# Gathers begin in the table's stage, table parts of 16 tokens, U chunks spread over V's loop

## The chip, the cores and the metric

The kernel runs on one core of a Trainium2 chip. The metric is device time in microseconds, from the first to the last instruction of one launch with what lies around them. Of several executions the median is taken.

## What is computed

One decoder layer for 512 tokens of width 1024, in float32: a sliding-window attention and an HGRN2 recurrence, merged, and then a PEER layer, which is what the change touches. For each token and each of 8 heads PEER finds 16 of 16384 experts by a product of two 128-key tables, with gates from a softmax. Each expert is one row of U and one row of V:

```python
def expert_block(args):
    ht, it, gt = args                       # tokens, expert numbers (128 a token), gates
    ue = jnp.take(u, it, axis=0)
    act = jax.nn.gelu(jnp.einsum('tkd,td->tk', ue, ht), approximate=False)
    ve = jnp.take(v, it, axis=0)
    return jnp.einsum('tk,tkd->td', gt * act, ve)
```

U and V have 16384 x 1024 elements, 64 MB each. The layer's output goes through a residual and a final RMS norm.

## The kernel before

**Two ways through PEER.** For 352 of the 512 tokens the kernel computes all experts densely. U comes in 128 chunks of 128 experts (`act_chunk`: a 512 KB load `s<-uc`, ScalarE makes `hi`, VectorE makes `lo`, PE does 24 matmuls of 128x352 at lines 642 to 645, ScalarE's Gelu at line 647 leaves 128 experts x 352 tokens in `gel`). The split in `hi` and `lo`, both of type fp32r, keeps the products' accuracy near float32. The gates stand in a table `Gd` in DRAM, expert by token, zero where a token did not choose the expert. V comes in 128 chunks as well: `w` is `gel` times the table (line 958), split in `whi` and `wlo`, and 18 matmuls of 512 columns (lines 972 to 974) add the chunk to six accumulators that stay in PSUM through the whole loop.

For the other 160 tokens the kernel gathers. 320 steps (`steps`, line 678) each fetch 128 rows, 512 KB, with an indirect DMA from GpSimd (line 687) into one of four `ga` buffers. A step on U takes a row's product with its token on VectorE (line 695); a step on V adds the row with its weight (line 705). `pace(goal, after)` issues gathers until `goal` have gone and puts each product two gathers behind.

**The stages.** Up to about 390 us the mixers run, then routing, in which 24 U chunks fill PE. From 612 to 782 us comes the table's stage (lines 873 to 897): for 8 tokens at a time VectorE makes one-hots `oh` in four operations, PE multiplies them (line 891, 16 matmuls), ScalarE moves the result to `G_`, and every 32 tokens (a part, 2 MB, 11 in all) SP writes the part to `Gd`. Between them U chunks are slotted in by `fill`. The buffers `gel` hold 53 chunks (`KEEP`); of these 50 are asked for before the read of the table's first slice (`g_load`), three after it (`LASTU`). Then comes V's loop (line 951): each of 128 steps does one V chunk, one U chunk as long as there are any, and gathers in proportion to PE's work. So the first 75 steps have a U chunk each and the last 53 have none.

**What sets the order.** The program is recorded in the order of the code, and a scheduler places each instruction on its engine's queue by a model of readiness, recorded order deciding between those that are ready; `issue_after` binds an instruction behind another, `keep_in_program_order` keeps the gathers in theirs. On the chip each engine takes its queue strictly in order. Buffers that matter: three for U loads (`s`), two for V loads (`vr`), two for `hi` and `lo`, which U and V share, two for `oh`, two for `G_`, four for `ga`, two PSUM banks for U chunks. SP's queue issues all loads and the table's writes.

## Time and profile before

| | us |
|---|---|
| median of three runs | 1681.73 (1674.09 to 1688.14) |
| profiled execution, its own time | 1682.85 |
| its span, first to last instruction | 1680.8 |
| PE busy | 1612.4 (96%) |
| VectorE busy | 1316.3 (78%) |
| ScalarE busy | 712.5 (42%) |
| GpSimd busy | 472.3 (28%) |
| moved by DMA | 400.88 MB, mean 238 GB/s |

An engine's busy share over the whole span hides stages with different limits, so the rows below are taken stage by stage. PEclk is the granted clock of PE as a share of full speed. The DMA share is the mean over 16 DMA engines; around 1.00 they are saturated. A wait is put down to what came last.

### The profile page before, as it was taken

How to read it: one execution, taken by the hardware profiler on the slowest of the kernel's cores; microseconds unless marked ns; L12 is line 12 of the kernel's file. 1: busy time of each engine (PE TensorE's matmuls, PEld its weight loads, DVE VectorE, ACT ScalarE, POOL GpSimd, SP SyncE). 2: the span in 40 equal slices, each digit the busy share in tenths (PEclk: the TensorE clock that was granted, in tenths of full speed). 3: DMA queues.
4: the chain of work that ended last, by engine and by line, in shares of the span. 5: the costliest groups of instructions: out<-in, count | busy, mean ns of one | idle time of the engine just before them, and what ended most of it. 6: DMA issues, size and time to landing. Idle time of an engine off the chain costs nothing.

```text
span 1680.8 us, 23572 instructions
## 1 busy us (share of the span) xinstructions
PE 1612.4 (96%) x8511; PEld 1357.3 (81%) x8511; DVE 1316.3 (78%) x2560; ACT 712.5 (42%) x1152; POOL 472.3 (28%) x341
## 2 busy tenths in 40 slices
PE   8999999999999989998899999999999999998997
PEld 6867678888989889997788888888888888776665
DVE  8466663647999988784888888888888887987788
ACT  5433352345455567775333333333333333333334
POOL 4000000000000000001455555555555554554442
PEclk9999999999999999999899999999999999999999
DMA  5311133324333236668999999999999998899985
GB/s 172 113 39 51 51 113 113 113 104 142 118 107 116 103 102 201 207 201 247 350 356 347 353 359 357 358 337 362 380 363 358 354 346 298 324 341 345 336 312 192
DMA packets 152260, 400.88 MB, mean 238 GB/s; under 512 B 13056, under 2 KB 60672, under 8 KB 152144
## 3 DMA queue, kind: packets, MB, share of 16 engines
q1 hardware_dynamic: 104064, 229.09, 39.8%
q0 software_dynamic: 46336, 168.39, 26.4%
q10 hardware_dynamic: 1744, 1.91, 0.4%
q8 instruction: 66, 1.08, 0.3%
q14 instruction: 50, 0.41, 0.1%
HBM read 371.91 MB, written 27.39 MB: 238 GB/s over the span
## 4 chain that ended last, share of the span: by engine, by line
PE 60%; DVE 15%; DMA 13%; issue 7%; POOL 3%; ACT 2%; DVEq 0%; ACTq 0%; SPq 0%; POOLq 0%
PE b L973 6%; PE b L974 6%; PE b L972 6%; PE b L642 5%; PE b L645 5%; PE b L643 5%; PE b L891 5%; DMA ga<-un,idx 5%; DMA vr<-vc 5%; PE b L262 4%; PE b L261 4%; DVE lo L161 4%; PE b L264 4%; DMA ga<-v,idx 3%; POOL ga L687 2%
## 5 line engine op out<-in xcount | busy, mean ns | idle before, releaser
L687 POOL DMA_INDIRECT ga<-un,idx x160 | 220.3, 1377 | 948.4 <-DMA s<-uc 753.0
L642 PE MATMUL b<-hT,hi 128*128 128x352 f32 x1024 | 330.2, 326 | 1.4 <-ACT hi L141 0.9
L643 PE MATMUL b<-hT,hi 128*128 128x352 f32 x1024 | 331.1, 325 | 0.0
L973 PE MATMUL b<-lo,whi 128*128 128x512 f32 (+1 forms) x768 | 307.6, 401 | 21.6 <-DVE lo L161 21.5
L972 PE MATMUL b<-hi,whi 128*128 128x512 f32 (+1 forms) x768 | 305.4, 399 | 19.1 <-ACT hi L141 18.9
L141 ACT ACTIVATE hi<-s 128x1024 fp32r<-128x1024 f32 (+1 forms) x195 | 205.8, 1056 | 264.9 <-PE b L643 161.4
L974 PE MATMUL b<-hi,wlo 128*128 128x512 f32 (+1 forms) x768 | 304.6, 397 | 0.0
L687 POOL DMA_INDIRECT ga<-v,idx x160 | 230.5, 1441 | 219.5 <-DVE e L705 202.6
L161 DVE TENSOR_TENSOR lo<-s,hi 128x1024 fp32r<-128x1024 f32 (+1 forms) x195 | 239.0, 1226 | 33.4 <-ACT hi L141 29.2
L141 ACT ACTIVATE whi<-w 128x352 fp32r<-128x352 f32 x128 | 63.5, 497 | 384.2 <-PE b L973 333.7
L705 DVE SCALAR_TENSOR_TENSOR e<-ga,wt,e 128x1024 f32<-128x1024 f32 x158 | 202.3, 1281 | 15.0 <-DMA ga<-v,idx 14.8
L695 DVE SCALAR_TENSOR_TENSOR dscr<-ga,h 128x1024 bf16<-128x1024 f32 x160 | 195.5, 1222 | 21.3 <-DMA ga<-un,idx 21.1
L642 PEld LDWEIGHTS b<-hT,hi 128*128 128x128 f32 x1024 | 193.1, 189 | 7.7 <-ACT hi L141 1.2
L973 PEld LDWEIGHTS b<-lo,whi 128*128 128x128 f32 (+1 forms) x768 | 139.4, 181 | 71.9 <-DVE lo L161 35.7
L643 PEld LDWEIGHTS b<-hT,hi 128*128 128x128 f32 x1024 | 193.4, 189 | 4.0
L645 PE MATMUL b<-hT,lo 128*128 128x352 f32 x1024 | 194.9, 326 | 0.0
L972 PEld LDWEIGHTS b<-hi,whi 128*128 128x128 f32 (+1 forms) x768 | 138.9, 181 | 58.6 <-ACT hi L141 25.0
L161 DVE TENSOR_TENSOR lo<-vr,hi 128x1024 fp32r<-128x1024 f32 x128 | 156.3, 1221 | 26.9 <-ACT hi L141 26.7
L974 PEld LDWEIGHTS b<-hi,wlo 128*128 128x128 f32 (+1 forms) x768 | 139.1, 181 | 38.9
L645 PEld LDWEIGHTS b<-hT,lo 128*128 128x128 f32 x1024 | 168.0, 189 | 0.0
L141 ACT ACTIVATE hi<-vr 128x1024 fp32r<-128x1024 f32 x128 | 134.3, 1049 | 65.7 <-DMA vr<-vc 64.4
L262 PE MATMUL b<-hT,hi 128*128 128x512 f32 (+1 forms) x376 | 146.5, 391 | 0.3 <-DVE hT L144 0.3
(286 smaller groups left out, 2170.9 us busy)
## 6 DMA issues: line engine op xcount, KB each, us to landing
s<-uc SPq DMA_DIRECT2D x128, 512.0 KB, 5.9
vr<-vc SPq DMA_DIRECT2D x128, 512.0 KB, 6.3
Gd<-G SPq DMA_DIRECT2D x11, 2048.0 KB, 9.4
gt<-Gd SPq DMA_DIRECT2D x32, 704.0 KB, 7.8
s<-wfm SPq DMA_DIRECT2D x30, 512.0 KB, 3.2
s<-wq SPq DMA_DIRECT2D x16, 512.0 KB, 3.3
s<-wmg SPq DMA_DIRECT2D x8, 512.0 KB, 3.3
s<-wout SPq DMA_DIRECT2D x8, 512.0 KB, 3.3
```

Source lines behind the costliest of these rows:

```text
L141: ACT.activation(dst, src, AF.Copy)
L161: (eng or V).tensor_tensor(lo[:, m], raw[:, m], hi[:, m].bitcast(F32), op=OP.subtract)
L262: PE.matmul(b, wh[:, k, :], rl(i), start=False, stop=False)
L642: PE.matmul(o, wh[:, k, :], zh[:, k, t], start=k == 0, stop=False)
L643: PE.matmul(o, wh[:, k, :], zl[:, k, t], start=False, stop=False)
L645: PE.matmul(o, wl[:, k, :], zh[:, k, t], start=False, stop=k == KD - 1)
L687: tc.keep_in_program_order(POOL.indirect_dma_start(out=t, out_offset=None, in_=a[src], in_offset=bass.IndirectOffsetOnAxis(ap=b.idx[:, j:j ...
L695: V.scalar_tensor_tensor(cur["scr"], t, 1.0, h20, op0=OP.mult, op1=OP.mult, accum_out=b.act[:, j:j + 1])
L705: V.scalar_tensor_tensor(b.ax, t, b.wt[:, j:j + 1], b.ax, op0=OP.mult, op1=OP.add)
L972: PE.matmul(acc[tb][hf][0:m, :], whi[:, t], vh[:, d], start=i == 0, stop=False)
L973: PE.matmul(acc[tb][hf][0:m, :], whi[:, t], vl[:, d], start=False, stop=False)
L974: PE.matmul(acc[tb][hf][0:m, :], wlo[:, t], vh[:, d], start=False, stop=i == NE - 1)
```

## The change

Five things are changed together.

- A part of the table has 16 tokens instead of 32 (`TG`): 22 writes of 1 MB, and in each the piece that lies together in DRAM is 256 bytes long instead of 512. `G_` shrinks by half.
- Gathers begin in the table's stage: the `ga` buffers have a pool of their own, opened before it, and `pace` is called after each part (one gather for two parts) and once with the goal 18 ahead of V's loop. The product with U's rows overwrites the gathered tile, in float32; before, it went to a scratch tile in bfloat16.
- U chunks are spread evenly over the first 116 steps of V's loop (`UEND`), and the share of gathers follows the count of V and U chunks.
- `FILLQ` 4 lets a U chunk follow every fourth quad of tokens instead of every fifth; `HELD` 5 and `LASTU` 2 change how many of the 53 chunks come where.
- The U chunks after the table are bound behind the last table matmul, the last two of them behind the issue of the table's first read as well, and V's first two loads are recorded ahead of that read.

```diff
@@ -37,7 +37,7 @@
 EQB = 1
 GS = 4096.0
 GC = 4
-TG = 32
+TG = 16
 QT = 4
 OT = 8
 LOOK = 26
@@ -48,11 +48,13 @@
 GLAG = 2
 GB = 4
 TAILC = 2
-HELD = 7
-LASTU = 3
+HELD = 5
+LASTU = 2
+EARLY = 18
+UEND = 116
 TL = 2
 F1 = 1.5
-FILLQ = 5
+FILLQ = 4
 
 
 def host(inp):
@@ -683,7 +685,7 @@
 
         def gather(i):
             b, src, j = steps[i]
-            t = cur["late"].tile([P, D], F32, tag="ga", bufs=GB, name=nm("ga"))
+            t = cur["ga"].tile([P, D], F32, tag="ga", bufs=GB, name=nm("ga"))
             tc.keep_in_program_order(POOL.indirect_dma_start(
                 out=t, out_offset=None, in_=a[src], in_offset=bass.IndirectOffsetOnAxis(ap=b.idx[:, j:j + 1], axis=0)))
             gq.append(t)
@@ -692,7 +694,7 @@
             t = gq.pop(0)
             b, src, j = steps[i]
             if src == "un":
-                V.scalar_tensor_tensor(cur["scr"], t, 1.0, h20, op0=OP.mult, op1=OP.mult, accum_out=b.act[:, j:j + 1])
+                V.scalar_tensor_tensor(t, t, 1.0, h20, op0=OP.mult, op1=OP.mult, accum_out=b.act[:, j:j + 1])
                 if j == b.w - 1:
                     ACT.activation(b.act, b.act, AF.Gelu)
                     V.tensor_tensor(b.wt, b.act, b.gate, op=OP.mult)
@@ -848,6 +850,7 @@
                 p_, c_ = slice(r * X, (r + 1) * X), slice(r * XG, (r + 1) * XG)
                 SP.dma_start(sp1.idx[p_, :], idxt[0:X, c_])
                 SP.dma_start(sp1.gate[p_, :], gta[0:X, 1, c_])
+        cur["ga"] = ps.enter_context(tc.tile_pool(name="gap", bufs=1, reuse_waits="tile"))
         cur["gel2"] = ps.enter_context(tc.tile_pool(name="gel2", bufs=1, reuse_waits="tile"))
 
 
@@ -883,21 +886,21 @@
                     V.tensor_tensor(oh[:, 0], ioq, row(iT[:, 0, t]), op=OP.is_equal)
                     V.tensor_tensor(oh[:, 2], ioq, row(iT[:, 1, t]), op=OP.is_equal)
                     V.tensor_tensor(oh[:, 1], oh[:, 2], row(g16[:, 0, t]), op=OP.mult)
-                    V.tensor_tensor(oh[:, 2], oh[:, 2], row(g16[:, 1, t]), op=OP.mult)
+                    last = V.tensor_tensor(oh[:, 2], oh[:, 2], row(g16[:, 1, t]), op=OP.mult)
                     for q in range(NQ):
                         b = bank((P, QT, P))
                         for i in range(QT):
                             for w in range(2):
-                                PE.matmul(b[:, i, :], oh[:, 0, q, :, i], oh[:, 1 + w, q, :, i], start=w == 0, stop=w == 1)
+                                lastg = PE.matmul(b[:, i, :], oh[:, 0, q, :, i], oh[:, 1 + w, q, :, i], start=w == 0, stop=w == 1)
                         m = o * OT + q * QT
                         ACT.activation(G_[:, :, m:m + QT].rearrange("p c t -> p t c"), b, AF.Copy)
                         k = (s_ * TG + m) // QT
                         if k % FILLQ == FILLQ - 1 and nu[0] < KEEP - HELD:
                             fill(1)
                 SP.dma_start(Gd.rearrange("g p s f -> s p g f")[s_], G_.rearrange("p (g c) t -> p g (c t)", c=GC))
+                pace((s_ + 1) // 2, last.ins)
         late = ps.enter_context(tc.tile_pool(name="late", bufs=1, reuse_waits="tile"))
         cur["late"] = late
-        cur["scr"] = late.tile([P, D], mybir.dt.bfloat16, name="dscr")
 
         acc = [[bank() for _ in range(2)] for _ in range(DB)]
         fold = late.tile([P, X], F32, name="fold")
@@ -914,13 +917,16 @@
         def g_load(g):
             if g < NE // GC:
                 gts[g] = late.tile([P, NPT, GC * TG], F32, tag="gt", bufs=2, name=nm("gt"))
-                SP.dma_start(gts[g], Gd[g])
-
-        fill(KEEP - nu[0] - LASTU)
-        g_load(0)
+                return SP.dma_start(gts[g], Gd[g])
+
+        with tc.issue_after(lastg.ins):
+            fill(KEEP - nu[0] - LASTU)
         for c in range(VPRE):
             v_load(c)
-        fill(LASTU)
+        g0 = g_load(0)
+        pace(EARLY, last.ins)
+        with tc.issue_after(lastg.ins), tc.issue_after(g0.ins):
+            fill(LASTU)
 
         def scale_of(ss, n):
             r = oc.tile([P, 1], F32, tag="ss", bufs=8, name=nm("rs"))
@@ -932,10 +938,11 @@
 
         def final_rows(y, add, t, n):
             s2_ = oc.tile([P, 2], F32, tag="s2_", bufs=4, name=nm("s2_"))
+            sq = s4([P, D])
             for hf in range(2):
                 d = slice(hf * 512, (hf + 1) * 512)
                 V.tensor_tensor(y[:, d], y[:, d], add[hf], op=OP.add)
-                ACT.activation(cur["scr"][0:n, d], y[:, d], AF.Square, accum_out=s2_[0:n, hf:hf + 1])
+                ACT.activation(sq[0:n, d], y[:, d], AF.Square, accum_out=s2_[0:n, hf:hf + 1])
             ss = oc.tile([P, 1], F32, tag="ss", bufs=8, name=nm("rs"))
             V.tensor_tensor(ss[0:n, :], s2_[0:n, 0:1], s2_[0:n, 1:2], op=OP.add)
             r = scale_of(ss[0:n, :], n)
@@ -945,9 +952,8 @@
                 (SP, ACT)[hf].dma_start(out[t:t + n, d], y[:, d])
 
         todo_u = NE - nu[0]
-        whole = 2.0 * todo_u + (NE - todo_u - TAILC)
+        nu0 = nu[0]
         ready = []
-        share = 0.0
         for c in range(NE):
             if c % GC == 0:
                 g_load(c // GC + 1)
@@ -973,8 +979,8 @@
                             PE.matmul(acc[tb][hf][0:m, :], whi[:, t], vl[:, d], start=False, stop=False)
                             PE.matmul(acc[tb][hf][0:m, :], wlo[:, t], vh[:, d], start=False, stop=i == NE - 1)
                 ready = []
-            share += 2.0 if nu[0] < NE else 1.0
-            fill(1)
+            fill(min(NE, nu0 + -(-todo_u * (c + 1) // UEND)) - nu[0])
+            share = (c + 1 + nu[0] - nu0) / (NE - TAILC + todo_u)
             if c == NE - 8:
                 ld = exp_ln_set()
                 yt = [e8([P, 2, D]) for _ in range(2)]
@@ -996,7 +1002,7 @@
                     bs.append(bank(tag="p"))
                     PE.matmul(bs[hf][0:X, :], fold[:, 0:X], sp1.ax[:, hf * 512:(hf + 1) * 512], start=True, stop=True)
                 final_rows(yx[0:X, :], [b[0:X, :] for b in bs], P, X)
-            pace(NS * share / whole, last.ins)
+            pace(EARLY + (NS - EARLY) * share, last.ins)
 
         while nsp[0] < NS:
             sparse(nsp[0])
```

Where the changed program's queues differ is shown at three places. Line numbers in its rows are those of the changed code (`s<-uc` at 153, `Gd` at 900).

SP's queue as the table's stage begins, before (`s` a U load, `Gd` a part's write):

```order
L849 DMA idx_3081<-idxt 32x32 x4
L151 DMA s_1103_6349<-uc 128x1024
L151 DMA s_1117_6449<-uc 128x1024
L897 DMA Gd<-G_5609 128x32x128
L151 DMA s_1130_6544<-uc 128x1024
L897 DMA Gd<-G_5744 128x32x128
L151 DMA s_1143_6642<-uc 128x1024
L151 DMA s_1156_6737<-uc 128x1024
L897 DMA Gd<-G_5912 128x32x128
```

The same place of the changed program:

```order
L851 DMA idx_3081<-idxt 32x32 x4
L900 DMA Gd<-G_5612 128x32x64
L900 DMA Gd<-G_5697 128x32x64
L900 DMA Gd<-G_5784 128x32x64
L900 DMA Gd<-G_5869 128x32x64
L900 DMA Gd<-G_5956 128x32x64
L900 DMA Gd<-G_6041 128x32x64
L900 DMA Gd<-G_6129 128x32x64
L153 DMA s_1097_6265<-uc 128x1024
L900 DMA Gd<-G_6214 128x32x64
L153 DMA s_1110_6353<-uc 128x1024
```

Before, U loads stand between the writes from the first part on; now seven writes stand in a row, and from there on loads and writes alternate. On PE the same shows as a stretch without U chunks, from the 22nd to the 41st of the 88 quads of tokens; 45 chunks precede the last table matmul, before it was 51.

VectorE's queue at the end of the table's stage, before (`lo` a split, `ga` a gathered tile, `gt` the table's slice):

```order
L885 TENSOR_TENSOR oh_7266<-oh_7266,g_5518 128x1024
L886 TENSOR_TENSOR oh_7266<-oh_7266,g_5518 128x1024
L161 TENSOR_TENSOR lo_7602<-s_1276_7599,hi_7601 128x1024
L958 SCALAR_TENSOR_TENSOR w_7639<-gel_3136,gt_7529 128x352
L958 SCALAR_TENSOR_TENSOR w_7712<-gel_3233,gt_7529 128x352
L963 TENSOR_TENSOR wlo_7643<-w_7639,whi_7641 128x352
L695 SCALAR_TENSOR_TENSOR dscr,act_3079<-ga_7696,h_62 128x1024
```

And in the changed program:

```order
L889 TENSOR_TENSOR oh_7447<-oh_7447,g_5521 128x1024
L697 SCALAR_TENSOR_TENSOR ga_7163,act_3079<-ga_7163,h_62 128x1024
L697 SCALAR_TENSOR_TENSOR ga_7334,act_3079<-ga_7334,h_62 128x1024
L697 SCALAR_TENSOR_TENSOR ga_7505,act_3079<-ga_7505,h_62 128x1024
L697 SCALAR_TENSOR_TENSOR ga_7622,act_3079<-ga_7622,h_62 128x1024
L697 SCALAR_TENSOR_TENSOR ga_7625,act_3079<-ga_7625,h_62 128x1024
L163 TENSOR_TENSOR lo_7304<-s_1245_7301,hi_7303 128x1024
L697 SCALAR_TENSOR_TENSOR ga_7628,act_3079<-ga_7628,h_62 128x1024
L697 SCALAR_TENSOR_TENSOR ga_7631,act_3079<-ga_7631,h_62 128x1024
L697 SCALAR_TENSOR_TENSOR ga_7634,act_3079<-ga_7634,h_62 128x1024
L163 TENSOR_TENSOR lo_7391<-s_1257_7388,hi_7390 128x1024
L163 TENSOR_TENSOR lo_7475<-s_1268_7472,hi_7474 128x1024
```

Eight products with gathered rows now stand between the last one-hots and the splits of the U chunks that PE does next; before, the first product came after w.

ScalarE's queue between the table and V in the changed program (`e` are Gelu results, `b` PSUM banks):

```order
L143 ACTIVATE hi_7522<-s_1279_7520 128x1024
L143 ACTIVATE hi_7554<-s_1283_7552 128x1024
L143 ACTIVATE hi_7586<-s_1287_7584 128x1024
L649 ACTIVATE e_527_3073<-b_7526 128x352
L143 ACTIVATE whi_7717<-w_7715 128x352
L143 ACTIVATE whi_7792<-w_7790 128x352
L649 ACTIVATE e_527_3073<-b_7558 128x352
L143 ACTIVATE hi_7645<-s_1301_7643 128x1024
L143 ACTIVATE hi_7677<-s_1305_7675 128x1024
```

Three U chunks (7590, 7649 and 7681) still have their Gelu after V's two weight splits `whi`; before, all three Gelus of the last chunks stood ahead of them.

## Rows read from the trace of the kernel before

**Rows 1.** Busy time by stage; the first line names the columns (x: instructions).

```profile
core 0: us, PE busy (x) PEld busy (x) DVE busy (x) ACT busy (x) POOL busy (x), PEclk, DMA share, GB/s
611.80:781.60 169.80, 169.80 (x1239) 157.62 (x1238) 133.18 (x195) 121.68 (x132) 1.02 (x1) 1.00 0.62 193
790.40:803.20 12.80, 0.15 (x1) 0.00 (x0) 2.33 (x4) 2.37 (x5) 0.00 (x0) 0.66 0.96 335
803.20:900.00 96.80, 93.13 (x465) 80.44 (x466) 81.88 (x124) 33.50 (x45) 49.87 (x38) 0.96 0.93 348
900.00:1422.60 522.60, 513.00 (x2687) 449.33 (x2686) 443.91 (x583) 190.58 (x258) 288.98 (x206) 1.00 0.96 353
1422.60:1670.30 247.70, 232.85 (x960) 171.16 (x958) 209.69 (x248) 85.16 (x126) 109.40 (x77) 0.99 0.87 312
```

**Rows 2.** PE's timeline around the hole: start, us, instruction [idle before, releaser].

```profile
789.12 1.43 PE L645 MATMUL b<-hT,lo 128*128 128x352 f32 x8
803.22 1.65 PE L972 MATMUL b<-hi,whi 128*128 128x512 f32 x3 [12.67 <-ACT hi L141]
...
806.14 0.63 PE L973 MATMUL b<-lo,whi 128*128 128x512 f32 x1
806.57 0.63 PE L974 MATMUL b<-hi,wlo 128*128 128x512 f32 x1
```

**Rows 3.** The same view of SP's queue and of DVE in the hole.

```profile
783.14 0.38 SPq L897 DMA_DIRECT2D Gd<-G  x1
...
796.69 0.33 SPq L917 DMA_DIRECT2D gt<-Gd  x1
...
800.69 0.96 DVE L958 SCALAR_TENSOR_TENSOR w<-gel,gt 128x352 f32<-128x352 f32 x2 [16.42 <-DMA gt<-Gd]
```

**Rows 4.** Transfers of 775 to 812: count, size, median us from issue to landing.

```profile
Gd<-G SPq DMA_DIRECT2D x1, 2048.0 KB, 13.5
...
ga<-un,idx POOLq DMA_INDIRECT x8, 7.0
```

**Rows 5.** Table's stage, timelines of SP's queue, of DVE and of PE.

```profile
658.39 0.38 SPq L897 DMA_DIRECT2D Gd<-G  x1
...
673.92 0.38 SPq L897 DMA_DIRECT2D Gd<-G  x1
...
647.71 1.22 DVE L161 TENSOR_TENSOR lo<-s,hi 128x1024 fp32r<-128x1024 f32 x1
648.85 0.69 DVE L885 TENSOR_TENSOR oh<-oh,g 128x1024 f16<-128x1024 f16 x1
649.45 0.68 DVE L883 TENSOR_TENSOR oh<-iok,iT 128x1024 f16<-128x1024 f16 x1
...
776.04 1.82 PE L891 MATMUL b<-oh 128*128 128x128 f16 x14
777.61 0.41 PE L642 MATMUL b<-hT,hi 128*128 128x352 f32 x1
```

**Rows 6.** Two us while a table part is written: columns as in Rows 1.

```profile
662.40:664.40 2.00, 2.00 (x18) 1.85 (x17) 2.00 (x3) 1.01 (x3) 0.00 (x0) 1.00 0.95 290
```

**Rows 7.** PE's timeline in V's loop: first matmuls of V, U and V again.

```profile
1406.67 0.40 PE L972 MATMUL b<-hi,whi 128*128 128x512 f32 x1
...
1410.81 0.32 PE L642 MATMUL b<-hT,hi 128*128 128x352 f32 x1
...
1414.61 0.39 PE L972 MATMUL b<-hi,whi 128*128 128x512 f32 x1
```

**Rows 8.** All DMA of 900 to 1400, and of 1430 to 1660.

```profile
DMA packets 48065, 178.14 MB, mean 356 GB/s; under 512 B 5376, under 2 KB 5376, under 8 KB 48028
...
DMA packets 20238, 75.74 MB, mean 329 GB/s; under 512 B 2272, under 2 KB 2272, under 8 KB 20224
```

**Rows 9.** Waits of 1440 to 1660: us in total, times, longest.

```profile
ACT hi L141 <- DMA vr<-vc: 64.4, 33, 5.3
```

**Rows 10.** Costliest groups: the products with gathered rows of U.

```profile
L695 DVE SCALAR_TENSOR_TENSOR dscr<-ga,h 128x1024 bf16<-128x1024 f32 x160 | 195.5, 1222 | 21.3 <-DMA ga<-un,idx 21.1
```

## The prediction

> **What bounds the kernel now.** I read the busy time by stage first, then PE's timeline at the joints, then transfers and waits. The profiled execution took 1682.85 us, 1.1 above the median of the three runs, less than can be told apart; the sum is made against it. PE is busy in every stage but one [rows 1]: 169.8 of 169.8 us in the table's stage, next to nothing in the 12.8 us from 790.4 to 803.2, and most of V's loop. The hole is a chain [rows 2, 3, 4]: the last part of the table is issued at 783.14, lands 13.5 us later because four gathers and a U load share the engines, the first read is issued at 796.69, w begins at 800.69, the first V matmul at 803.22. After it PE starts at half clock: granted 0.66 over the hole [rows 1], matmuls 0.43 us apart instead of 0.23 [rows 2, 7].
>
> In V's loop a step's 18 V matmuls take 4.14 us and a U chunk's 24 take 3.80 at full clock [rows 7]. So 75 steps with a chunk would take 595.5 us and the 53 without 219.4, 814.9 together. They took 619.4 and 247.7 [rows 1], 867.1. The loss of 52.2 falls in three: 8.9 in the first 97 us (465 matmuls at 0.189 are 87.9), 14.6 or 2.8% up to 1422.6 (2687 matmuls are 508.0), and 28.3, or 0.53 a step, in the steps without U. The last has its own cause: there ScalarE waited 64.4 us for V's loads [rows 9]. Two buffers turn over in two steps of 4.14 us, too short for a load, a split and the wait in the queue.
>
> **The change, step by step.**
>
> *U over 116 steps instead of 75.* 41 of the 53 steps without U become steps in the mix; 12 stay. At full clock nothing changes, since the work is the same. For the loss I take three terms. The 12 bare steps lose 0.53 each: 6.4. For the start I take 6, between 2.2 less than before (eleven slow matmuls at 0.20 extra, if the hole goes) and half of 8.9. For the rest of the mix the question is the DMA engines. A step with U asked for a U and a V load (0.524 MB each), a quarter of a table read (0.18) and 3.18 gathers (1.67), 2.90 MB per 7.94 us or 365 GB/s; 356 were delivered [rows 8]. Spread out, and with 302 gathers left for 201 shares, a step asks for 2.34 MB per 6.60 us, 355 GB/s, just what was delivered. So its loss lies between 1% (jitter alone) and the old 2.8% with something on top for V loads that now follow each other closely; I take 2% of 670 us, 13, with 7 and 27 as ends. V's loop: 815 + 6 + 13 + 6 = 840, **27 less** than 867.1.
>
> *Gathers from the table's stage on.* All of 18 gathers, 0.524 MB each, leave V's loop; that is counted in the 355 above. Of the products on VectorE 16 come before V. Each is a group of 1.22 us [rows 10]; that the product overwrites its own tile in 32 bits instead of a 16-bit scratch I cost at nothing, as the split beside it writes 32 bits in the same 1.22 [rows 5], and 0.06 a piece would hide in VectorE's idle time (443.9 busy of 522.6 [rows 1]).
>
> *FILLQ, HELD and the order.* The order of the changed program has something the diff does not show. Before, U loads ran ahead of the table writes in SP's queue, and 51 chunks were done by the last table matmul. Now seven writes stand in a row ahead of the next U load, and PE's order has no chunk between quads 22 and 41 of the 88; 45 are done at the end. PE's work until V is the same, so only idle time counts. In that stretch VectorE makes 9.5 groups of one-hots at 4 x 0.60 us [rows 5] and three products, 26.6 us; PE needs 9.5 x 16 matmuls at 0.112 [rows 5], 17.0. VectorE can be ahead by two buffers, 4.8. PE idles about 5 us (0 to 10).
>
> *After the table.* Eight chunks, 30.4 us of PE, now stand between the last table matmul and V, where the way from that matmul (781.6) to V took 21.6 us. The old hole, 12.8 us, is covered. What is late next is VectorE: five products stand in its order ahead of the split for PE's first chunk, three more ahead of the second's, and SP's next U loads and the table's first read wait behind those splits. Four gathers can be in their buffers by then. The fifth is issued when the first product is done and takes 7.0 us [rows 4]: product 5 ends about 9.5 us in, the first split 10.7, while PE, whose last table matmul ends about 1.9 us in, has wanted it since 4.4. That is 6 us, and about 1 more at the next chunk: 7 (2 to 9, the low end if all gathers are early). ScalarE has two of V's weight splits, which wait for the table's read, ahead of the evacuation that chunk seven's bank needs; by my count the read lands as PE gets there. With 1 us for a lower clock the idle time before V is 5 + 7 + 1 = 13, against 12.8: **nothing gained up to V's start** (-8 to +6).
>
> *Table parts of 16 tokens.* 22 writes of 1 MB with 4096 pieces of 256 bytes replace 11 of 2 MB with 4096 of 512. While a part is written alone the engines move 290 GB/s [rows 6], 28.2 ns for a piece on one of 16. No row has a piece of 256 bytes. From below, half the time for half the bytes is 14.1 ns; from above, the same 28.2. Pieces of 4 KB at 356 GB/s take 184 ns [rows 8]; the straight line through the two gives 17.1 at 256 bytes, and I take that. A part is then 4.4 us on 16 engines. The stage, 153 us with 17 U loads and 11 gathers at 1.47 each, leaves 112 for 22 parts, 5.1 a piece or 19.9 ns per packet: it fits, narrowly. Cost 0. SP's issue, 0.38 us [rows 5], is idle time there.
>
> The Trainium skill (DMA: Bandwidth & Descriptors, Specifications) speaks against this part: below 512 B the engine reads, modifies and writes, and line rate is lost. No run here shows it; the page gives no price. By that rule the time of rival 1 or more would come out.
>
> Sum: 1682.85 - 27 + 0 = **1656 us**, own range 1638 to 1674.
>
> **Rivals.**
>
> 1. *The small pieces bind the table's stage; slower.* If a piece costs 28.2 ns whatever its size, a part takes 7.2 us, 22 take 159, and with 41 for the rest the engines need 200 us in a stage of 153: 47 more, 1703 us. The price decides from 24.7 ns, where 22 parts cost the 27 us that V's loop gives. For it: each write is followed at once by PE work that needs its buffer (two of them), and 512-byte pieces already move at 290 where pieces of 4 KB move at 356, so part of a piece's price does not shrink with it. Against it: the line above. Chance 0.20, and in half of that the piece costs more than 28.
>
> 2. *Spread-out U makes V loads late.* With 116 V's to 75 U's, 41 times two V's follow each other, with two buffers as before. If each such pair loses what a bare step lost, 41 x 0.53 = 22 comes back: 1678, no change. Against it: a chunk before or after the pair gives the load some 12 us, where a bare pair gave 8.3. Chance 0.17.
>
> 3. *More than forecast.* The gathers are early, VectorE holds nobody, V's mix loses 1%: 13 - 7 and another 8 to 13: about 1637. Chance 0.11.
>
> My forecast has 0.52. **Numbers.** About 1% is what a measurement can tell from no change. Faster than 1665: most of 0.52 and rival 3, 0.55. Within 1% (to 1698.5): the forecast's upper tail, rival 2 and the cheaper half of rival 1, 0.31. Slower: the dearer half of rival 1 and accidents, 0.14. The range 1637 to 1700 leaves out the worst of rival 1 and a little below.
>
> **What would show it.** PE's idle before the first V matmul gone, but waits for "lo" some 2 to 10 us after the last table matmul; a stretch of the table's stage in which PE is busy three quarters; the time from issue to landing of a table part, 7 to 9 us if right, over 11 and DMA at its limit through the stage if rival 1 holds; bare steps 12 instead of 53, and ScalarE's wait for V's loads under 20 us in all. V's loop at 840 from first to last matmul is the step on which the forecast stands; at 860 rival 2 holds. I am wrong if the table's stage from first to last matmul takes more than 165.

## The result and the profile after

The changed kernel took 1700.03 us (median of 4 runs, 1699.69 to 1701.04) against 1681.9 for the kernel before, a ratio of 1.0111, 95% interval 1.0069 to 1.0154: about 1% slower, 44 us above my forecast of 1656. The profiled execution took 1699.82 with a span of 1697.0, 16.2 longer than the span before.

Busy time by stage of the changed kernel, with the columns of rows 1: the table's stage, the way from it to V, V's loop; then three stretches of the table's stage and 3 us in which little but a table part is written.

```profile
615.70:808.40 192.70, 171.29 (x1102) 156.63 (x1101) 139.96 (x212) 99.12 (x116) 13.98 (x13) 0.84 0.66 181
808.40:853.00 44.60, 35.21 (x196) 34.09 (x194) 24.23 (x33) 18.25 (x24) 13.25 (x11) 0.89 0.98 331
853.00:1686.70 833.70, 824.63 (x4108) 697.53 (x4108) 707.17 (x908) 305.65 (x428) 426.58 (x299) 1.00 0.93 342
...
615.70:667.00 51.30, 45.75 (x336) 41.69 (x336) 40.33 (x62) 32.62 (x36) 2.09 (x2) 0.87 0.61 164
667.00:692.00 25.00, 19.85 (x150) 18.70 (x149) 21.83 (x35) 11.87 (x14) 2.30 (x2) 0.78 0.87 231
692.00:808.40 116.40, 105.69 (x619) 96.25 (x616) 77.79 (x116) 54.62 (x67) 9.60 (x9) 0.84 0.64 178
...
745.00:748.00 3.00, 3.00 (x11) 3.00 (x11) 1.62 (x3) 0.00 (x0) 0.00 (x0) 0.50 0.82 217
```

Against [rows 1]: the first table matmul comes 3.9 us later (615.7), the table's stage is 22.9 longer (192.7), the way from it to V 23.0 longer (44.6 instead of 21.6), V's loop 33.4 shorter (833.7). The sum is +16, which is what the spans say. V's loop came out as forecast; the table's stage did not, 192.7 instead of 153. PE was idle there for 21.4 us, and its 171.3 busy us hold work that takes about 148 at full clock (an estimate: the forecast's 153 less its 5 of idle time); the granted clock was 0.84 on the mean.

The timeline of SP's queue shows the order taking hold (start, us, engine, line; a long duration is time in which the queue's next issue waited):

```profile
623.65 43.09 SPq L900 DMA_DIRECT2D Gd<-G  x7
666.83 4.09 SPq L153 DMA_DIRECT2D s<-uc  x1
672.68 0.36 SPq L900 DMA_DIRECT2D Gd<-G  x1
...
809.73 9.25 SPq L153 DMA_DIRECT2D s<-uc  x1
819.81 0.36 SPq L900 DMA_DIRECT2D Gd<-G  x1
```

Seven writes in 43 us, in which no U load is issued. From there one write and one U load take turns, and a part takes 10.6 us (eleven in the 116.4 from 692 on). What I had costed at nothing is this turn-taking. One period of it, timelines of PE, ScalarE, VectorE and SP's queue:

```profile
738.51 3.70 PE L894 MATMUL b<-oh 128*128 128x128 f16 x30
739.06 3.77 ACT L896 ACTIVATE G<-b 128x512 f32<-128x512 f32 x4
742.44 0.28 PE L894 MATMUL b<-oh 128*128 128x128 f16 x1 [0.23 <-DVE oh L888]
742.61 1.08 ACT L143 ACTIVATE hi<-s 128x1024 fp32r<-128x1024 f32 x1
...
742.89 0.27 PE L894 MATMUL b<-oh 128*128 128x128 f16 x1 [0.17 <-ACT G L896]
743.32 4.08 SPq L153 DMA_DIRECT2D s<-uc  x1
743.74 0.66 PE L644 MATMUL b<-hT,hi 128*128 128x352 f32 x1 [0.58 <-ACT hi L143]
744.20 0.49 PE L645 MATMUL b<-hT,hi 128*128 128x352 f32 x1
744.50 0.49 PE L644 MATMUL b<-hT,hi 128*128 128x352 f32 x1
...
750.38 3.72 PE L894 MATMUL b<-oh 128*128 128x128 f16 x30
752.24 0.69 DVE L886 TENSOR_TENSOR oh<-iok,iT 128x1024 f16<-128x1024 f16 x1 [5.59 <-PE b L894]
```

PE makes all 32 matmuls of a part in one block and a whole U chunk in the next. While the chunk runs, VectorE has both one-hot buffers full and waits 5.59 us for PE; when PE turns to the table, it uses them up and waits for the next. ScalarE evacuates four banks before it makes the chunk's hi, so PE waits for that too. The three waits are 0.23, 0.17 and 0.58 us. After them the matmuls stand 0.30 us apart instead of 0.16: granted clock 0.50, which is 1.2 GHz, for most of the chunk (6.64 us from 743.74 to 750.38, where 3.80 is full clock [rows 7]). This chunk is one of the two slowest. The other seven from 711 to 793 took 5.2 to 5.6 us, with half the clock for 9 to 12 of their 24 matmuls, and the two at 693.5 and 702.7 took 3.9, at full clock, though such waits stand ahead of them too. The turns of those two chunks took 9.2 and 9.1 us.

The U load is not what is late. Counted in their order, the hi made at 742.61 belongs to the load issued at 722.12. It stands in ScalarE's queue behind the Gelu of the chunk before it, which waits for that chunk's last matmul, and behind the four evacuations. So it is not made while PE works on that chunk, though ScalarE idles 5.6 to 6.9 us in that time. In the kernel before, PE's order mixed the two kinds finely, 14 table matmuls and then some of U [rows 5], and idled nowhere.

PE's timeline behind the table shows the same on the way to V: the four waits before U chunks, 9.4 us in all. ScalarE's timeline below it shows the second and the third: hi comes behind the Gelu (`e`) of the chunk before, the second also behind the table's last four evacuations.

```profile
810.16 0.43 PE L644 MATMUL b<-hT,hi 128*128 128x352 f32 x1 [1.51 <-ACT hi L143]
...
820.69 0.66 PE L644 MATMUL b<-hT,hi 128*128 128x352 f32 x1 [4.88 <-ACT hi L143]
...
828.13 0.43 PE L644 MATMUL b<-hT,hi 128*128 128x352 f32 x1 [1.50 <-ACT hi L143]
...
833.87 0.43 PE L644 MATMUL b<-hT,hi 128*128 128x352 f32 x1 [1.50 <-ACT hi L143]
...
815.84 0.46 ACT L649 ACTIVATE e<-b 128x352 f32<-128x352 f32 x1 [5.73 <-PE b L647]
816.20 3.58 ACT L896 ACTIVATE G<-b 128x512 f32<-128x512 f32 x4
819.58 1.06 ACT L143 ACTIVATE hi<-s 128x1024 fp32r<-128x1024 f32 x1
826.67 0.46 ACT L649 ACTIVATE e<-b 128x352 f32<-128x352 f32 x1 [6.03 <-PE b L647]
827.03 1.05 ACT L143 ACTIVATE hi<-s 128x1024 fp32r<-128x1024 f32 x1
```

The hole of [rows 2] is gone. In V's loop ScalarE's waits for V's loads, which were 64.4 us in the steps without U alone [rows 9], are 22.0 us in all (waits of 860 to 1687: us, times, longest):

```profile
ACT hi L143 <- DMA vr<-vc: 22.0, 9, 4.7
```

### The profile page after: what moved, and what is told of

Same layout as the page of the kernel before. It is cut to its first block, busy times and chain, and to the rows that moved or that the text cites. A ratio compares the mean times of both kernels' runs of the same rounds, so it can differ in the third digit from the quotient of the medians.

```text
span 1697.0 us, 23476 instructions
## 1 busy us (share of the span) xinstructions
PE 1628.2 (96%) x8511; PEld 1380.5 (81%) x8511; DVE 1316.2 (78%) x2560; ACT 699.6 (41%) x1152; POOL 476.6 (28%) x341
## 4 chain that ended last, share of the span: by engine, by line
PE 51%; issue 19%; DVE 13%; POOL 11%; DMA 4%; ACT 1%; POOLq 0%; DVEq 0%; SPq 0%; ACTq 0%
POOL ga L689 10%; PE b L979 6%; PE b L980 5%; PE b L978 5%; PE b L264 4%; PE b L263 4%; PE b L266 4%; PE b L644 4%; PE b L645 4%; PE b L647 3%; DVE lo L163 3%; DMA ga<-v,idx 2%; PE b L894 2%; DMA vr<-vc 1%; DVE ti L840 1%
## 5 line engine op out<-in xcount | busy, mean ns | idle before, releaser
L644 PE MATMUL b<-hT,hi 128*128 128x352 f32 x1024 | 343.7, 339 | 18.8 <-ACT hi L143 18.3
L645 PE MATMUL b<-hT,hi 128*128 128x352 f32 x1024 | 341.8, 336 | 0.0
L979 PE MATMUL b<-lo,whi 128*128 128x512 f32 (+1 forms) x768 | 302.9, 394 | 9.1 <-DVE lo L163 8.8
L978 PE MATMUL b<-hi,whi 128*128 128x512 f32 (+1 forms) x768 | 301.9, 394 | 0.0
L689 POOL DMA_INDIRECT ga<-v,idx x160 | 235.1, 1470 | 207.0 <-DVE e L707 181.9
L644 PEld LDWEIGHTS b<-hT,hi 128*128 128x128 f32 x1024 | 203.3, 199 | 32.0 <-ACT hi L143 25.5
L697 DVE SCALAR_TENSOR_TENSOR ga<-ga,h 128x1024 f32<-128x1024 f32 x160 | 194.4, 1220 | 20.6 <-DMA ga<-un,idx 20.3
L645 PEld LDWEIGHTS b<-hT,hi 128*128 128x128 f32 x1024 | 203.8, 199 | 4.0
L647 PE MATMUL b<-hT,lo 128*128 128x352 f32 x1024 | 188.5, 325 | 0.0
```

The lines of the kernel that those rows point to most:

```text
L644: PE.matmul(o, wh[:, k, :], zh[:, k, t], start=k == 0, stop=False)
L645: PE.matmul(o, wh[:, k, :], zl[:, k, t], start=False, stop=False)
L647: PE.matmul(o, wl[:, k, :], zh[:, k, t], start=False, stop=k == KD - 1)
L689: tc.keep_in_program_order(POOL.indirect_dma_start(out=t, out_offset=None, in_=a[src], in_offset=bass.IndirectOffsetOnAxis(ap=b.idx[:, j:j ...
L697: V.scalar_tensor_tensor(t, t, 1.0, h20, op0=OP.mult, op1=OP.mult, accum_out=b.act[:, j:j + 1])
L978: PE.matmul(acc[tb][hf][0:m, :], whi[:, t], vh[:, d], start=i == 0, stop=False)
```

## Experiments

Theory 1: the 16-token parts change the order (a run of writes ahead of U's loads, then U and table in lock-step), and in that order PE's short waits halve its clock. Theory 2: the DMA engines are the limit in the table's stage (my rival 1). Theory 3: the early gathers and their products hold things up. The measure is the time from the first table matmul to the first V matmul, in which PE has the same work in the kernel before and in the change. It has less in e3, e4, e10 and e11, which leave chunks to V's loop; in e8, e13 and e14 two and a half chunks that else stand ahead of the table fall into it, so there the time of the first V matmul is compared. Times are medians, ratios are to the kernel before with their 95% interval. The other columns are of the one profiled execution of each; executions of one kernel differ by up to 15 us (the kernel before: 1674 to 1690 in 25 executions), so a few us in these columns say little.

| kernel | us | ratio | table to V | clock in table's stage | V's loop |
|---|---|---|---|---|---|
| before | 1681.9 | | 191.4 | 1.00 | 867.5 |
| changed | 1700.0 | 1.011 (1.007-1.015) | 237.3 | 0.84 | 834.1 |
| e1 parts of 16 alone | 1719.4 | 1.022 (1.019-1.026) | 237.0 | 0.77 | 858.1 |
| e2 no early gathers | 1714.6 | 1.019 (1.015-1.024) | 235.9 | 0.82 | 858.5 |
| e3 room for 14 | 1705.9 | 1.014 (1.011-1.018) | 235.6 | 0.85 | 845.6 |
| e4 room for 14, 512 B | 1674.7 | 0.996 (0.994-0.998) | 200.0 | 0.89 | 850.6 |
| e5 spread alone | 1667.2 | 0.993 (0.990-0.995) | 192.2 | 1.00 | 851.8 |
| e6 early, not spread | 1710.7 | 1.017 (1.015-1.020) | 236.6 | 0.84 | 847.5 |
| e7 filler matmuls | 1685.0 | 1.003 (1.001-1.005) | 223.1 | 0.94 | 834.6 |
| e8 as e4, U to the end | 1677.0 | 0.998 (0.997-1.000) | 202.8 | 0.92 | 853.9 |
| e9 parts of 32, no early | 1678.9 | 0.998 (0.996-1.000) | 197.1 | 0.96 | 861.2 |
| e10 parts of 32, early | 1684.9 | 1.003 (1.000-1.005) | 202.9 | 0.87 | 863.1 |
| e11 as e4, not bound | 1676.0 | 0.997 (0.995-0.999) | 195.0 | 0.97 | 857.3 |
| e12 8 written, 4 read | 1692.2 | 1.006 (1.004-1.008) | 207.3 | 0.95 | 856.3 |
| e13 chunk bound | 1722.0 | 1.025 (1.020-1.029) | 263.0 | 0.82 | 841.2 |
| e14 filler in the wait | 1695.5 | 1.009 (1.006-1.012) | 237.9 | 0.97 | 834.8 |

**Which part of the change costs.** e1 is the kernel before with one line edited; e2 is the change without the gathers of the table's stage.

```
e1:  -TG = 32                      e2:  -EARLY = 18
     +TG = 16                           +EARLY = 0
                                        -                pace((s_ + 1) // 2, last.ins)
```

> The kernel before with parts of 16 tokens and nothing else of the change: no early gathers, U not spread. The measure is the time from the first table matmul to the first V matmul, in which PE's work is the same in all three kernels (24 U chunks and the table): 191.4 us before, 237.3 changed. Theory 1 (the order: with 16-token parts nine table writes stand in SP's queue ahead of the next U load, then U chunks and parts run in lock-step, in which PE idles a little and its clock falls): 220 to 240 us here too, the whole run 1700 to 1715. Theory 2 (the DMA engines are the limit, 256-byte pieces): 200 to 230, and DMA share over 0.9 through the table's stage. Theory 3 (the early gathers and their products on VectorE hold up the one-hots and U's loads): 180 to 192, the whole run 1670 to 1682.

> The change without its early gathers (none are issued before V's loop, all 318 are shared out over it); parts of 16 tokens, U spread, the bound loads stay. SP's and PE's order in the table's stage are the change's. Theory 1 (order): first table matmul to first V matmul 225 to 238 us (237.3 in the change; a few less, since no products of VectorE stand ahead of the splits after the table), V's loop 838 to 845 with 18 more gathers in it, the whole run 1695 to 1705. Theory 2 (DMA engines): 16 us less traffic, 220 and 1685. Theory 3 (gathers): 190 to 200, the whole run 1655 to 1668.

Both took what the change took, 237.0 and 235.9; the whole runs came out 4 and 10 us over the expected. The table's stage of each, columns as above:

```profile
610.90:785.60 174.70, 146.67 (x1006) 135.44 (x1005) 123.36 (x184) 94.72 (x108) 0.00 (x0) 0.77 0.57 148
```

```profile
611.20:801.60 190.40, 161.52 (x1102) 153.95 (x1101) 127.35 (x188) 99.08 (x116) 1.64 (x2) 0.82 0.59 160
```

Theory 3 falls: with next to no gather in the stage the loss is the same. Theory 2 has the DMA engines busy 0.57 and 0.59 of it, where it asked for 0.9. e2's V loop missed my expectation (838 to 845) by 13 us or more; e5 and e6 take that up.

**The size of a piece.** e3 leaves room for 14 later chunks, three fewer; e4 does that and puts 8 experts in a table row, which makes a piece 512 bytes and, by that alone, gives back an order in which U's loads run among the writes.

```
e3, e4:  -LATE = 17      e4:  -GC = 4
         +LATE = 14           +GC = 8
```

> The change with room for 14 instead of 17 later U chunks, so 50 instead of 53 are made before V: the other half of a pair with the next kernel. Three chunks of 3.8 us move behind V's start. Theories 1 to 3 all say: first table matmul to first V matmul 226 us (237.3 less 11.4), V's loop 845, the whole run 1695 to 1703.

> As the kernel with room for 14, with 8 instead of 4 experts to a table row: a part of 16 tokens goes out as 2048 pieces of 512 bytes instead of 4096 of 256, and a table read is 2 MB. The gathers and everything else of the change stay. In SP's order U loads now stand among the writes from the first part on (at most two writes in a row until 45 chunks are made; then nine writes without a U load). Theory 1 (order): first table matmul to first V matmul 180 to 190 us against 226, the whole run 1650 to 1665. Theory 2 (engines): 22 parts at 28.2 ns a piece, 1.2 us less each, so 26 less: 200, the whole run 1674. Theory 3 (gathers): 226 as in its pair, 1700.

e3 missed: with three chunks less it should have taken 226 from table to V and took 235.6, since U's loads behind the table came late and PE idled 21.4 us in one wait for hi. The pair differs by 31 us in the whole run and 35.6 from table to V. But 200.0 and 1674.65 are theory 2's numbers, not theory 1's. The windows of e4 tell why I do not read them so: up to 715 PE never idles and has its full clock, and the loss is in the last stretch, in which no U chunk is left and PE waits for one-hots at a clock of 0.55, with the engines at 0.74, and behind the table in one wait of 12.9 us for hi. That is an argument; e7, e13 and e14 below test it.

```profile
690.00:715.00 25.00, 25.00 (x182) 23.61 (x180) 20.68 (x30) 16.71 (x19) 1.33 (x2) 1.00 0.83 243
...
740.00:760.00 20.00, 12.42 (x98) 11.08 (x99) 17.45 (x29) 11.74 (x13) 1.15 (x1) 0.55 0.74 211
```

**U's chunks up to the stage's end.** e8 is e4 with FILLQ 5 and each fill bound behind an earlier table matmul.

```
+                        gl.append(lastg.ins)
                         if k % FILLQ == FILLQ - 1 and nu[0] < KEEP - HELD:
-                            fill(1)
+                            with tc.issue_after(gl[max(0, k - 12)]):
+                                fill(1)
```

> As the kernel with pieces of 512 bytes and room for 14 (1674.65 us; first V matmul at 811.7), but the U chunks of the table's stage are one to every five groups of eight matmuls and each load may not be issued before the table matmul 12 groups back: the scheduler can no longer run U ahead, and chunks stand among the groups up to the end (43 at the 80th of 88). There the clock fell to 0.55 to 0.64 in the last 37 us, in which no U chunk was left and PE waited for one-hots. Theory 1 in its present form (PE keeps its clock in the table's stage only where U chunks stand between the groups; else VectorE's one-hots bound it): clock over 0.95 through the stage, first V matmul 10 to 16 us earlier, at 796 to 802, the whole run 1659 to 1665. If the DMA engines set the stage: no change, 811 and 1675.

It missed. The first V matmul came at 811.8, as in e4, and the clock was 0.92. The stage ended at 777.0 (777.4 in e4), with the same products and one-hots on VectorE, which was busy for 139 us of it in both; and behind it V's first loads, a read of 1.44 MB (not 2, as the expectations of e4 and e11 have it), U's loads and the last early gathers share engines that are busy all the time (1.02 at 415 GB/s from 790 to 815). So a better clock (0.92 instead of 0.89) did not bring the end forward here. e11 is e4 without the bindings of U's last loads:

```
-        with tc.issue_after(lastg.ins):
-            fill(KEEP - nu[0] - LASTU)
+        fill(KEEP - nu[0] - LASTU)
...
-        with tc.issue_after(lastg.ins), tc.issue_after(g0.ins):
-            fill(LASTU)
+        fill(LASTU)
```

> As the kernel with pieces of 512 bytes and room for 14 (1674.65; first V matmul at 811.7), but U's loads after the table are bound neither behind the last table matmul nor behind the table's first read. The scheduler then puts 50 chunks ahead of the 80th group and only one behind the table. If the bound loads cost time there (the one wait of 12.9 us for hi): first V matmul at 795 to 803, the whole run 1659 to 1667. If they fill a hole that is there anyway (the table's last part and a first read of 2 MB, with V's first loads, at 415 GB/s): an idle stretch of 12 to 20 us before V, first V matmul at 808 to 816, the whole run 1671 to 1679.

The first V matmul came at 806.9, between the two expectations, with an idle stretch of some 15 us ahead of it, and V's loop gave the gain back: 1675.95, no different from e4. The bound loads fill a hole and are late by about as much.

**Whether the waits halve the clock.** e7 puts five filler matmuls ahead of each chunk of the table's stage. The scheduler set them among the table's matmuls, where they filled the wait only in part, and the stretch without U shrank too; the pair e13 and e14 mends that. In both a chunk's matmuls follow the table matmul that they follow in the program, one chunk after every four groups; in e14 five fillers stand right ahead of it.

```
e7:   +            for k in range(dummy):
      +                PE.matmul(o, zh[:, k, 0:P], zh[:, k, t], start=k == 0, stop=k == dummy - 1)
e13:  +            with (tc.issue_after(cur["lastg"]) if bind else contextlib.nullcontext()):
      +              for k in range(KD):
                       PE.matmul(o, wh[:, k, :], zh[:, k, t], start=k == 0, stop=False)
e14:  +                with tc.issue_after(cur["lastg"]):
      +                    for k in range(dummy):
      +                        PE.matmul(o, zh[:, k, 0:P], zh[:, k, t], start=k == 0, stop=k == dummy - 1)
```

> The change with five matmuls more ahead of each of the 22 U chunks that are made within the table's stage, into the same PSUM bank, on operands that have long been there, and overwritten by the chunk's own first matmul: PE has work while it would wait for the chunk's hi. They are 110 matmuls, 17.6 us at 0.16. In the change the table's stage and the way to V took 237.3 us, of which 12 are idle waits for hi and about 30 are matmuls at half clock. If it is the short waits that bring the clock down: the clock in the stage goes from 0.84 to 0.93 or more, and the 237.3 become 215 to 228 in spite of the added work. If the clock falls for another reason, or the DMA engines set the pace of a part: 245 to 260, clock 0.82 to 0.86.

> The change with the matmuls of each of the table stage's U chunks bound behind the table matmul that they follow in the program: one chunk after every four groups nearly from the first group on; five writes in a row at the start instead of seven, the stretch of PE's order without U is 4 groups (24 to 28) instead of 19. 26 instead of 29 chunks stand ahead of the first table part's end, so the measure is the time of the first V matmul (853.0 in the change). If the lock-step costs what it did in the change (10.5 us a part instead of 7.5): 850 to 870, clock in the table's stage 0.80 to 0.88, the whole run 1697 to 1715. If most of the loss was the stretch without U: 825 to 840, clock over 0.92, the whole run 1672 to 1687.

> The same with five filler matmuls right ahead of each chunk (110 in all, 17.6 us at 0.16; overwritten by the chunk's first matmul), bound behind the same table matmul as the chunk was in the last kernel: they run in PE's wait for hi. Transfers and pieces are the same. If the short waits bring the clock down: clock in the table's stage 0.95 or more, first V matmul no later than in the last kernel in spite of 17.6 us more work, and by 10 to 30 us earlier if that one was at 850 or more. If the clock is low for another reason, or the DMA engines set the pace: first V matmul 8 to 20 us later than in the last kernel.

e7 gained 14 us from table to V in spite of its fillers, with the same transfers, so the engines' time was not the limit: theory 2 falls. e13 took 1722, with the first V matmul at 871.8, both a little over what was expected of the lock-step; from 669 on it holds in every turn, and a turn takes 10.9 to 12.4 us. e14 has 106 matmuls more in the table's stage, yet that is 27.9 us shorter, and V starts 24.2 earlier, at 847.6. Against the change that is 5.4 us earlier, with 17 us more work for PE. The table's stage of each, and PE's timeline at a chunk, e13 first:

```profile
608.80:834.60 225.80, 197.30 (x1184) 184.39 (x1183) 144.44 (x215) 107.41 (x125) 13.45 (x13) 0.82 0.60 168
```

```profile
719.95 0.40 PE L896 MATMUL b<-oh 128*128 128x128 f16 x2 [1.39 <-DVE oh L890]
720.60 0.66 PE L646 MATMUL b<-hT,hi 128*128 128x352 f32 x1 [0.25 <-ACT hi L143]
...
726.99 3.72 PE L896 MATMUL b<-oh 128*128 128x128 f16 x30
```

```profile
609.70:807.60 197.90, 184.51 (x1290) 173.53 (x1290) 144.63 (x215) 108.65 (x125) 12.47 (x12) 0.97 0.68 189
```

```profile
720.24 1.05 PE L646 MATMUL b<-hT 128*128 128x352 f32 x5
721.88 0.40 PE L898 MATMUL b<-oh 128*128 128x128 f16 x2 [0.58 <-DVE oh L892]
722.55 0.43 PE L648 MATMUL b<-hT,hi 128*128 128x352 f32 x1 [0.27 <-ACT hi L143]
...
726.47 3.71 PE L898 MATMUL b<-oh 128*128 128x128 f16 x30
```

Without fillers PE is idle for 1.64 us ahead of the chunk and then needs 6.39 for it, 18 of its 24 matmuls 0.29 apart; with them it is idle for 0.85 and needs 3.92, at 0.16. The chunk and its loads are the same. Over e13's 14 turns from 669 on a chunk takes 5.8 on the mean (5.2 to 6.6), in e14's turns 3.8 to 3.9, so the waits cost somewhat more through the clock (1.9 us a turn) than in themselves (1.6).

e13 holds a second comparison. Its second to fifth turns have the same two blocks, 32 table matmuls and then a whole chunk, and the same 16-token parts, yet PE neither idles nor loses its clock in them, and a turn takes 7.6 us. ScalarE's queue differs there: the hi of a chunk to come stands ahead of this chunk's Gelu. The four turns, and ScalarE in the first of them:

```profile
619.70:650.20 30.50, 30.50 (x225) 29.82 (x224) 23.74 (x35) 19.54 (x22) 0.00 (x0) 1.00 0.51 132
...
626.25 1.06 ACT L143 ACTIVATE hi<-s 128x1024 fp32r<-128x1024 f32 x1 [1.51 <-PE b L647]
627.47 0.47 ACT L651 ACTIVATE gel<-b 128x352 f32<-128x352 f32 x1 [0.16 <-PE b L649]
628.48 3.87 ACT L898 ACTIVATE G<-b 128x512 f32<-128x512 f32 x4 [0.53 <-PE b L896]
```

So the block order by itself costs nothing; it costs where nothing is ready for the next block. These turns also have no gather and no U load beside them, and no run moves hi alone, so this last step is argued and not shown.

**What shortened V's loop.** e5 is the kernel before with U spread over 116 steps, e6 the change without that.

```
e5:  -            fill(1)
     +            fill(min(NE, nu0 + -(-todo_u * (c + 1) // UEND)) - nu[0])
e6:  -            fill(min(NE, nu0 + -(-todo_u * (c + 1) // UEND)) - nu[0])
     +            fill(1)
```

> The kernel before with U's 75 chunks spread over 116 steps of V's loop and nothing else of the change. My forecast gave this step 27 us (841 in V's loop from 867.5), since bare steps wait for V's loads. The rival that the last runs suggest: V's loop is set by what the DMA engines must move in it (867.5 us at 341 GB/s before, 858.5 at 342 without early gathers but with the spread, 834.1 at 342 in the change), so the gathers that leave it bring the gain, and the spread alone little. By my step: V's loop 841 to 848, the whole run 1655 to 1663. By the rival: 858 to 867, the whole run 1672 to 1682.

> The change with one U chunk in every step of V's loop until none is left, as before; the early gathers stay. By my step (spread brings the gain): V's loop 855 to 862 against the change's 834.1, the whole run 1720 to 1728. By the rival (the bytes that leave V's loop): 834 to 842, the whole run 1700 to 1708.

The two together make what the change has. V's loop by itself, e5 and then e6:

```profile
803.90:1655.70 851.80, 833.02 (x4108) 699.30 (x4108) 737.95 (x954) 305.14 (x428) 447.74 (x320) 1.00 0.94 347
```

```profile
851.60:1699.10 847.50, 831.95 (x4109) 699.20 (x4108) 708.44 (x908) 309.11 (x428) 418.02 (x299) 0.99 0.92 336
```

The spread alone takes 15.7 us off 867.5 (e5); the change takes 33.4 off. e6's 20.0 are not those of the early gathers alone, as it has the 16-token parts too, and these by themselves gave 9.4 (e1, 858.1). V starts later with them, and nine gathers instead of four have been issued before it; in the change and in e6 it is 26 (for V's loop the two rows above count 320 and 299 GpSimd instructions), so some 22 leave V's loop and not 18. The shares do not add up: against e1 the spread gives nothing (e2, 858.5), against e6 it gives 13.4, and the early gathers give 10.6 without it (e1 to e6) and 24.4 with it (e2 to the change). In both runs the loop came out between the two expectations. e5 is also the fastest kernel of all, 1667.2, a ratio of 0.993 (0.990 to 0.995): it keeps the order of the table's stage.

**Keeping both gains.** Three tries at early gathers or covered holes without the bad order. e9 is the change with parts of 32 and no early gathers; e10 has 18 early gathers in two buffers and room for 12 chunks; e12 is the change with 8 experts in a written row, of which a read takes 4.

```
e9:   -TG = 16     e10:  -TG = 16           e12:  +GW = 8
      +TG = 32           +TG = 32                 -    Gd = dr.tile([NE // GC, P, NPT, GC * TG], F32, name="Gd")
      -EARLY = 18        -LATE = 17               +    Gd = dr.tile([NE // GW, P, NPT, GW * TG], F32, name="Gd")
      +EARLY = 0         +LATE = 12               -                return SP.dma_start(gts[g], Gd[g])
                         +GE = 2                  +                return SP.dma_start(gts[g], Gd[r][:, :, f:f + GC * TG])
```

> The change with parts of 32 tokens, as before, and without early gathers: U spread, the bound U loads and the other small edits stay. SP's and PE's order in the table's stage are those of before; 48 chunks are done by the 80th of 88 groups and five stand behind the table, whose loads wait for the last table matmul, two of them for the table's first read as well. Theory 1 (only the 16-token parts' order costs time): the table's stage takes 168 to 172 us, V's loop 850 to 854 as with the spread alone, and the hole of 12.8 us before V is filled by three more chunks: first V matmul at 790 to 797, the whole run 1653 to 1661. If the bound loads come too late behind the table's read, as in the kernel with pieces of 512 bytes (one wait of 12.9 us): first V matmul at 800 to 806, the whole run 1664 to 1670, the same as the spread alone (1667.2).

> As the last kernel but with the 18 early gathers, one per part of the table's stage, in two buffers of their own; they take the room of five later U chunks, so 48 instead of 53 are made before V (5 x 3.8 = 19 us of PE move into V's loop), and no chunk is left for the last 40 of the 88 groups. Early gathers take 20 us off V's loop by the runs so far (867.5 to 847.5 without the spread, 851.8 to 834.1 with it). If they cost nothing in the table's stage: V's loop 853, first V matmul at 785 to 792, the whole run 1650 to 1657. If PE's wait for one-hots in the last 40 groups brings the clock down there, as in the kernel with pieces of 512 bytes (0.55 to 0.64 in its last 37 us): first V matmul at 795 to 805, the whole run 1660 to 1670.

> The change with one thing different: a row of the table in DRAM holds 8 experts instead of 4, so a part goes out as 2048 pieces of 512 bytes; a read still takes 4 experts, 0.72 MB in pieces of 256 bytes. Room for 17 later chunks, 53 before V, gathers, spread and bound loads are the change's. In SP's order at most two writes stand in a row until 48 chunks are made at the 72nd group; five chunks stand behind the table. Theory 1 (the order that 4096 pieces of 256 bytes called for, with U and table in lock-step and the clock halved): first table matmul to first V matmul 195 to 205 us instead of 237.3 (the kernel with room for 14 took 200.0 with three chunks less, but its last 28 groups had no U; here 16), V's loop 834 to 840, the whole run 1658 to 1668. If 256-byte pieces mattered only by the time that the engines take for them (22 parts, 1.2 us each): 211 and 1674. If neither: 237 and 1700.

e9's stage took 165.8, but V started at 809.5, later than either expectation. SP's queue behind the last write shows it (e9): the load of a constant waits 9.45 us, most likely for memory that the last part still holds (not shown; in the kernel before a part landed 9.4 us after its issue on the median). V's loads, the table's read and U's bound loads stand behind it, and PE idles 9.1 us in a wait for hi.

```profile
779.41 0.36 SPq L899 DMA_DIRECT2D Gd<-G  x1
779.81 9.45 SPq L905 DMA_DIRECT2D fold<-const  x1
789.36 3.45 SPq L911 DMA_DIRECT2D vr<-vc  x2
793.34 0.91 SPq L153 DMA_DIRECT2D s<-uc  x2
```

e10 lost its gain in the stretch without U, as its second expectation had it (first V matmul at 816.4, clock 0.87), and more. e12 took 207.3 to V instead of 237.3, at a clock of 0.95; that lies between theory 1's 195 to 205 and the 211 of a price in engine time alone, and does not decide between them. Its whole run missed, as its expectation held an error: in the change a read takes a whole row, 5632 bytes per partition in one piece, and only in e12 does it go in pieces of 256 bytes, 90112 of them. V's loop, with nearly the same order in every queue, shows the price, 856.3 instead of 834.1:

```profile
824.00:1680.30 856.30, 834.68 (x4110) 700.98 (x4108) 709.52 (x910) 303.85 (x428) 421.57 (x300) 0.99 0.97 334
```

```profile
ACT hi L144 <- DMA vr<-vc: 77.0, 27, 7.9
```

## Why the prediction was wrong, step by step

**V's loop: right in the sum.** 840 forecast, 833.7 measured; ScalarE's wait was 22.0 where under 20 was forecast. PE was busy for 824.6 of it. Both the spread and the gathers that left the loop carried it (e5, e2), but not in shares that these runs settle, and 22 gathers left where I had counted 18. Three kernels with the spread and without early gathers (e2, e5, e9) have loops from 851.8 to 861.2; those 9 us stay unexplained, and executions of one kernel differ by as much.

**The table's stage: wrong, and this decided.** The step that failed is "PE idles about 5 us (0 to 10)" together with the silence on what follows quad 41. The stretch without U, which I had read from the order, cost 10.7 us of idle time (51.3 and 25.0 us with 45.75 and 19.85 busy) instead of 5. And I took the turn-taking of writes and U loads behind it for a steady state without loss, a term at nothing. It took 10.6 us a part where the same work without waits takes 7.6 (e13's early turns). About half of the 3 us are the waits and what goes with them (the two turns at full clock took 9.2 and 9.1), the other half is the lower clock. Of the 45 us above full-clock work in this stage, 21 are idle time and some 23 are lost in matmuls that ran slower, most of it at half clock. I had read the clock after the hole of 12.8 us [rows 1, 2] and priced it there, and not asked whether waits under 1 us would do the same. e1 and e2 show that the loss comes with the 16-token parts alone, e13 and e14 that filling the waits restores the clock. The Trainium skill (TensorE: Matmul & The Clock Gate, A second HAM failure mode: psum-queue depth-cycling) tells of frequent short idles between groups of matmuls by which the clock swings between its levels; e13 and e14 agree, with 0.82 and 0.97 in the stage.

**The way to V: the sign right, the cause not.** I forecast 37.4 us (30.4 of U and 7 of idle time); it took 44.6, 9.4 idle and the rest at a clock of 0.89. I had VectorE's products hold up the splits; without products ahead of them e2 took 45.5. PE waited for hi, not for lo as I had it: 1.5 us twice while ScalarE made the Gelu of the chunk before and then hi, 1.5 at first behind evacuations of the table, and 4.9 where the table's last four evacuations stood between Gelu and hi. The U load that waits 9.25 us in SP's queue does not hold the last table write behind it, which goes out at 819.81, as those evacuations end (819.78).

**Pieces of 256 bytes: right.** While a part is written alone the engines moved 217 GB/s at a share of 0.82, 18.9 ns a piece on one of 16, of which 15.5 busy; I took 17.1 between 14.1 and 28.2. The time in which a part lands, one of my signs, stands in no row of the changed kernel. Rival 1 gave 1703 and the run took 1700, but that nearness is luck, as the mechanism was another: it had the engines at their limit, and they were busy 0.66 of the stage. The rule of the Trainium skill that I weighed (DMA: Bandwidth & Descriptors, Specifications) shows as 217 GB/s against 290 for 512 bytes [rows 6], not as a doubling. What the small pieces did, they did in the order that the scheduler chose: with 512 bytes (e4, e12) it set U's loads among the writes again.

**The start.** The first table matmul came 3.9 us late. The kernels without early gathers had it at 610.9 to 612.4, those with them at 608.8 to 616.7; I have not followed it further.

## What to carry to other kernels

When a change moves an order, compare not only how much work there is. Where two blocks of matmuls take turns, look in the queues of the engines that feed PE whether the next block's operands are made while this one runs (e13's early turns, 7.6 us) or only behind its result (10.6 to 12.4). Waits of some tenths of a microsecond at every turn came with half the clock for much of the next block, so they cost about twice what the idle time shows. Where such waits cannot be taken away, filler matmuls on old operands are worth trying: e7 was 15 us faster than the change and e14 26 faster than e13, but e14's 4.5 against the change lie within the intervals. And look at what one edit does to the order alone before costing the rest: here one number of six cost 46 us from table to V (e1), more than the 33 that V's loop gained by everything together.

## What the runs showed that I had not expected

A granted clock of 0.50 came after waits of 0.2 to 0.6 us (0.98 in a turn of some 10.6), though not after the first such turns; with 0.85 us of idle time in a turn of 9.7 and fillers in the rest of the wait (e14) it stayed at full. Reads of the table in 90112 pieces of 256 bytes instead of 4096 of 5632 cost V's loop 22 us, where as many writes of 256 bytes in the table's stage kept the engines at two thirds. And gathers taken out of V's loop gave back less than their bytes take: the 17 of 0.524 MB by which the change's loop has fewer than e2's take 26.0 us at the loop's 342 GB/s, and the loop is 24.4 shorter with the spread, but only 10.6 without it (e1 to e6).
